# Where an odd tile's output projection transposes the next tile's inputs: behind two or behind three groups of products

## The chip, the cores and the metric

The kernel runs on one core of one Trainium2 chip. The time is that of one execution on the device, in microseconds (us), from several executions of which the median counts. The engines are named as in the profile: PE is TensorE (matrix products and transposes), ACT is ScalarE, DVE is VectorE, POOL is GpSimd, and SP is SyncE, which here only issues DMAs.

## The reference

The reference is one encoder layer over 2048 tokens of width 1024. Two kinds of attention give 512 columns each; these are normalised, joined and multiplied by one output matrix; the result is added to the residual stream; a router then picks two of 32 experts for each token, and their gated MLPs are added.

```python
mixed = concatenate([rmsnorm(out_a, g_out_a), rmsnorm(out_b, g_out_b)], axis=-1)
x = x + mixed @ w_out                                  # output projection, this change
h2 = rmsnorm(x, g_ffn_norm)
y = hierarchical_moe(h2, w_router_group, ..., w_gate, w_up, w_down)
x = x + y
return rmsnorm(x, g_final)
```

## The kernel before

The program is written out by hand: every engine executes its instructions in the order in which the code issues them, and an instruction whose input is not ready holds all that stands behind it on its engine. The change is in `phase5`, which does the output projection, the second norm and the routing, for 16 tiles of 128 tokens. Its loop body for tile n does pieces of several tiles:

- `proj(n)`: the products of tile n with the output matrix, two halves of 512 columns. Inputs and weights are split into a high and a low part, so each half takes three groups of eight products (high by high, high by low, low by high), six groups in all, numbered 1 to 6 here. `proj` is a generator; `ahead(pj, k)` issues the next k groups. The products are line L1425, with `mT_hi` or `mT_lo` as the input. The row of group 3 and of group 6 is thus one with `mT_lo`.
- `trans(n + 1)`: transposes the next tile's normalised inputs `ab` (PE, L1408, eight transposes, four to a PSUM tile), then takes each PSUM tile out in two steps: `mT_hi` on ACT (L1410) and `mT_lo` on DVE (L1411). `mT_hi` and `mT_lo` are needed by group 1 of the next tile.
- `trans2(n - 1)`: transposes the new residual stream of the tile before for the router (PE, L1477), taken out by ACT (L1483) and DVE (L1484) into `hT`.
- `resid`, `square`, `resid2`, `norm2`: residual addition (DVE, L1435), its squares (ACT, L1449), a Newton iteration for the inverse root (`nw`, first on DVE, then six small steps on POOL, L1295 and L1296), and the norm itself (DVE, L1466).
- `merge1` to `merge3`, `squares`, `rms`, `scale`: they make `ab` of later tiles. `rms` (a second Newton iteration, for two tiles, all on DVE, up to L1300) comes once in every even tile. `scale` (two ACT steps, L1353, one for each half of `ab`) writes `ab` of tile n + 2: in an even tile behind `rms`, near the end of the tile, in an odd tile right behind `trans2`. There is one `ab` buffer, so the next can be written only when the transposes have read the last.
- `logits` (even tiles, PE L1509 and L1511) and `route` (DVE steps, and POOL DMAs that write the routing table, L1616), dealt out a few steps at a time by `some(k)`. A table of four tiles starts in tiles 5, 9 and 13.

Both kinds of transposes take their PSUM tile from one pool `pt` (name `pT`) of two buffers, each holding four transposes:

```python
pt = cps.enter_context(tc.tile_pool(name="p5t", bufs=2, space=PSUM))
def ahead(it, k):
    for _ in range(k):
        next(it, None)
```

So the eight transposes of `trans` fill both buffers, and the eight of `trans2` behind them can start when DVE has finished the first `mT_lo`, and their second four when it has finished the second.

Of the kernel before, what the change touches and what calls it, by code (L numbers as in the profile page):

```python
# [36 lines left out]
class K:  # L37
# [1328 lines left out]
    def phase5(self):  # L1366
# [14 lines left out]
        with ExitStack() as ctx:  # L1381
# [15 lines left out]
            def load_x(c):  # L1397
                st[c]["x1"] = w2.tile([128, D], F32, name="x")
                nc.sync.dma_start(st[c]["x1"], x[c])

            def trans(c):
                d = st[c]
                ab = d.pop("ab")
                mT = d["mT"] = [wk.tile([128, 8, 128], F32R, name="mT_hi"), wk.tile([128, 8, 128], F32R, name="mT_lo")]
                for q in range(2):
                    ps = pt.tile([128, 4, 128], F32, name="pT")
                    for j in range(4):
                        nc.tensor.transpose(ps[:, j], ab[:, q, j], self.ident)  # L1408
                    sl = slice(4 * q, 4 * q + 4)
                    nc.scalar.activation(mT[0][:, sl], ps, AF.Copy)  # L1410
                    nc.vector.tensor_sub(mT[1][:, sl], ps, mT[0][:, sl])  # L1411

            def proj(c):

                d = st[c]
                mT = d.pop("mT")
                last = c == NT - 1
                t = [pm.tile([128, 2, 512], F32, name="pm") for _ in range(2 if last else 1)]
                d["ps"] = ps = [t[0][:, 0], t[1][:, 0]] if last else [t[0][:, 0], t[0][:, 1]]
                d["pt"] = t[0]  # L1420
                for half in range(2):
                    n = 0
                    for a, b in PASS:
                        for j in range(8):
                            nc.tensor.matmul(ps[half], mT[a][:, j], wo[b][j // 2][:, j % 2, 512 * half:512 * half + 512],  # L1425
                                             start=(n == 0), stop=(n == 23))
                            n += 1
                            if j == 7 or j == 3 and half and last:
                                yield

            def resid(c, half=None):
                d = st[c]
                x1 = d["x1"]
                if half is None:
                    nc.vector.tensor_add(x1, d["pt"].rearrange("p a b -> p (a b)"), x1)  # L1435
                else:
                    n = slice(512 * half, 512 * half + 512)
                    nc.vector.tensor_add(x1[:, n], d["ps"][half], x1[:, n])
                if half != 0:
                    nc.sync.dma_start(dr["x1"][128 * c:128 * c + 128], x1)  # L1440

            def square(c, half=None):
                d = st[c]
                if half is None:
                    d["h2"] = p.tile([128, 8, 128], F32, name="h2")
                if half != 1:
                    d["ssx"] = sm.tile([128, 2], F32, name="ssx")
                if half is None:
                    nc.scalar.activation(d["h2"].rearrange("p a b -> p (a b)"), d["x1"], AF.Square,  # L1449
                                         accum_out=d["ssx"][:, 0:1])  # L1450
                else:
                    nc.scalar.activation(d["ps"][half], d["x1"][:, 512 * half:512 * half + 512], AF.Square,
                                         accum_out=d["ssx"][:, half:half + 1])

            def resid2(c):
                d = st[c]
                ss = d.pop("ssx")
                if c == NT - 1:
                    nc.vector.tensor_add(ss[:, 0:1], ss[:, 0:1], ss[:, 1:2])
                d["rx"] = newton(ss[:, 0:1], 1.0 / D, sm, "nw2", last=c >= NT - 3)  # L1460
# [328 lines left out]
            def some(k):  # L1789

                nonlocal hold
                if hold:
                    hold -= 1
                    if hold:
                        return
                    if n == 14:
                        k = 100
                for _ in range(2 * k if 13 <= n < 15 else k):
                    if next(routes, None) == "pe":
                        hold = 4  # L1800
                        return

            def until(mark):
                nonlocal hold
                held, hold = hold, 0
                if held and mark == "pe":
                    return
                for m in routes:
                    if m is not None and m == mark:
                        break  # L1810
# [3 lines left out]
# [4 lines that stand above are left out]
            def finish_logits(n):  # L1818
                nonlocal routes
                for _ in lgs:  # L1820
                    pass
                g = {5: 0, 9: 1, 13: 2}.get(n)
                if g is not None:
                    until(None)
                    routes = chain(route(g), choose()) if g == 1 else route(g)
# [4 lines left out]
            def whole_w(e, m, t):  # L1830

                stages[e, 2 * m], stages[e, 2 * m + 1] = t[:, 0:1024], t[:, 1024:2048]
                gather(t, wsrc[m], self.idx2[:, e:e + 1])
# [38 lines left out]
            for n in range(NT - 1):  # L1872
                pj = proj(n)
                even = n % 2 == 0
                ahead(pj, 1)
                if n >= 1:
                    resid(n - 1)
                    square(n - 1)
                if not even and n >= 3:
                    finish_logits(n)  # L1880
                ahead(pj, 1)
                load_x(n)
                if even and n + 3 < NT:
                    load_ob(n + 3)
                if even and n + 2 < NT:
                    merge3(n + 2)
                    merge3(n + 3)
                some(4)
                trans(n + 1)
                if n >= 1:  # L1890
                    resid2(n - 1)
                some(4)
                if n == 12:
                    until(None)
                    whole_w(0, 0, self.slot(7, F32))
                    gu0 = [pA.tile([128, 4, 2, 256], F32R, name=f"a{i}") for i in range(4)]
                ahead(pj, 2)
                if n >= 1:
                    trans2(n - 1)
                if even and n + 2 < NT:  # L1900
                    squares(n + 2)
                    squares(n + 3)
                if n + 5 < NT:
                    load(n + 5)
                if not even and n + 2 < NT:
                    scale(n + 2)
                    if n + 3 < NT:
                        load_ob(n + 3)
                if n == 13:
                    half_split(0, 0, (gu0,), nc.vector)  # L1910
                if n == 14:
                    for i in (2, 3):
                        half_split(0, i, (gu0,), nc.vector)
                some(3)
                if n + 4 < NT:
                    merge1(n + 4)
                if n >= 1:
                    norm2(n - 1)
                some(2)
                if n + 4 < NT:  # L1920
                    merge2(n + 4)
                some(2)
                if even:
                    for _ in pj:
                        pass
                    if n >= 2:
                        lgs = logits(n - 1)
                        next(lgs)
                if even and n + 2 < NT:
                    rms(n + 2)  # L1930
                    scale(n + 2)
                if n == 13:
                    half_split(0, 1, (gu0,), nc.vector)
                if n == 13:
                    whole_w(0, 1, self.slot(7, F32))
                if n == 13:
                    for i in range(3):
                        half_w(1, i, self.stage())
                if n == 14:
                    until(None)  # L1940
                    first_rec()
                some(2)
                for _ in pj:
                    pass

            n = NT - 1
            pj = proj(n)
# [464 lines left out]
```

## Time and profile before

| what | value |
| --- | --- |
| time, median of 3 runs | 2306.95 us (2306.91 to 2308.32) |
| profiled execution, its own time | 2312.83 us |
| span of the profiled execution | 2310.6 us |
| PE busy, share of the span | 2060.5 us, 89% |
| DVE, ACT, POOL busy | 1666.5, 1439.9, 1092.7 us |
| the loop over tiles 0 to 15 | about 1500 to 1790 us of the span |

The span is counted from the first to the last instruction; the profiled execution's own time is 2.2 us longer, and it lies 5.9 us above the median of the runs without a profile. A change of the profiled execution is therefore carried over to the median as a difference. Rows of a timeline give the start, the duration, the engine, the line, the operation, output and inputs, the shape and a count where equal instructions are merged; in brackets stands how long the engine was idle before the row, and which instruction ended that. A PE row's duration reaches to the modelled end of its last product, which overlaps the start of the next row, so the time that a row takes is read from start to start.

### The profile page before, as it was taken

The page shows a single profiled execution, that of the slowest core. Times are in us where ns is not written, and L with a number is a line of the kernel's source. Part 1 is how long each engine was busy: PE and PEld are TensorE (multiplying, and loading weights), DVE is VectorE, ACT ScalarE, POOL GpSimd, SP SyncE. Part 2 cuts the span into 40 slices and gives each one's busy share as a digit, 9 for nine tenths or more (in the row PEclk, how much of TensorE's full clock was granted, in tenths as well). Part 3 has the DMA queues.
Part 4 walks back from the last instruction along what each step waited for, and adds up shares of the span by engine and source line. Part 5 has one row for each costly group of instructions (what it writes and reads, how often), then busy time and mean ns, then how long its engine had stood idle before and what let it go on. Part 6 is the DMA issues. An engine that isn't in the chain of part 4 may idle for free. (4 is left out here: it accounts for less than half of the span.)

```text
span 2310.6 us, 42905 instructions
## 1 busy us (share of the span) xinstructions
PE 2060.5 (89%) x16099; PEld 1458.3 (63%) x16099; DVE 1666.5 (72%) x3741; ACT 1439.9 (62%) x2125; POOL 1092.7 (47%) x1193
## 2 busy tenths in 40 slices
PE   5889989788889899999999999898888899999990
PEld 3458434577778466665655655577776588788870
DVE  7732221488887788888888899968787577777765
ACT  5532211499997588888888878744343366667653
POOL 1110000377763255555555556644654656667740
PEclk9989989999999899999999999899998999999995
DMA  4412344956735100000000221154444789999978
GB/s 153 131 54 68 123 151 122 224 139 153 163 100 154 37 20 22 6 22 21 7 22 9 55 93 24 34 165 143 150 147 147 219 298 293 291 308 319 311 211 308
DMA packets 196676, 312.81 MB, mean 135 GB/s; under 512 B 64185, under 2 KB 149090, under 8 KB 183460
## 3 DMA queue, kind: packets, MB, share of 16 engines
q1 hardware_dynamic: 166420, 174.43, 26.4%
q0 software_dynamic: 29760, 134.85, 18.2%
q8 instruction: 127, 2.08, 0.4%
q14 instruction: 81, 0.66, 0.1%
q10 hardware_dynamic: 288, 0.79, 0.1%
HBM read 235.66 MB, written 101.25 MB: 146 GB/s over the span
## 5 line engine op out<-in xcount | busy, mean ns | idle before, releaser
L961 POOL TENSOR_TENSOR lo<-p,hi 128x512 f16<-128x512 f32 x256 | 343.0, 1344 | 295.5 <-ACT p L955 233.7
L954 ACT ACTIVATE hi<-S,mla_scale 128x1024 f16<-128x1024 f32 x256 | 285.5, 1115 | 135.0 <-PE S L949 133.4
L923 DVE TENSOR_REDUCE part<-M 128x1 f32<-128x512 f32 x512 | 340.4, 680 | 13.1 <-PE M L921 11.7
L955 ACT ACTIVATE p<-S,mla_scale 128x1024 f32<-128x1024 f32 x256 | 285.2, 1114 | 0.0
L960 DVE TENSOR_TENSOR lo<-p,hi 128x512 f16<-128x512 f32 x256 | 228.9, 895 | 12.1 <-ACT p L955 10.3
L983 PE MATMUL O<-VB,lo 128*128 128x65 f16 x2048 | 198.9, 194 | 6.8 <-DVE lo L960 4.3
L978 PEld LDWEIGHTS <-hi 128*128 128x128 f16 x2048 | 184.9, 98 | 27.0 <-issue 21.5
L978 PE MATMUL O<-VB,hi 128*128 128x129 f16 (+1 forms) x2048 | 198.9, 215 | 0.0
L983 PEld LDWEIGHTS <-lo 128*128 128x128 f16 x2048 | 177.7, 99 | 17.4 <-DVE lo L960 5.9
L729 POOL TENSOR_TENSOR pp<-sb,st 128x256 f32<-128x256 f32 (+1 forms) x256 | 142.9, 581 | 45.1 <-DVE st L706 32.9
L2117 DVE TENSOR_TENSOR s<-raw,s 128x1024 fp32r<-128x1024 f32 x120 | 140.2, 1221 | 17.1 <-ACT s L2115 16.0
L1425 PE MATMUL pm<-s,mT_hi 128*128 128x512 f32 x512 | 137.3, 415 | 3.8 <-ACT mT_hi L1410 3.8
L2074 PE MATMUL pd<-s,hT 128*128 128x512 f32 x540 | 138.2, 404 | 1.7 <-ACT hT L2061 1.7
L614 POOL TENSOR_SCALAR t<-t,a_scale 128x512 f32<-128x512 f32 (+1 forms) x12 | 16.1, 1354 | 261.3 <-DMA t<-d_r 245.2
L2161 POOL DMA_INDIRECT d_x<-o,rec x47 | 88.1, 1874 | 106.7 <-ACT s L2115 33.7
L365 DVE SCALAR_TENSOR_TENSOR qk_sb<-pm,wscale,qk_sb 128x512 f16<-128x512 f32 x32 | 24.0, 750 | 149.3 <-ACT qk_sb L364 149.3
L746 PE MATMUL PT<-ident,pp 128*128 128x128 f32 (+1 forms) x640 | 104.5, 287 | 25.6 <-ACT pp L733 24.0
L2115 ACT ACTIVATE s<-raw 128x1024 fp32r<-128x1024 f32 x120 | 118.2, 1049 | 12.8 <-DMA raw<-in_w_up,eidx 6.8
L733 ACT ACTIVATE pp<-pp,a_scale 128x512 f32<-128x512 f32 (+1 forms) x160 | 114.0, 713 | 11.2 <-POOL pp L729 9.5
L2074 PEld LDWEIGHTS pd<-s,hT 128*128 128x128 f32 x540 | 101.2, 188 | 30.1 <-issue 4.3
L364 ACT ACTIVATE qk_sb<-pm,wscale 128x512 f16<-128x512 f32 x32 | 22.0, 688 | 153.4 <-DMA d_qk<-qk_sb 76.8
L1425 PEld LDWEIGHTS pm<-s,mT_hi 128*128 128x128 f32 x512 | 98.8, 198 | 26.1 <-ACT mT_hi L1410 4.1
(511 smaller groups left out, 5963.7 us busy)
## 6 DMA issues: line engine op xcount, KB each, us to landing
x<-in_x SPq DMA_DIRECT2D x32, 512.0 KB
na<-d_na SPq DMA_DIRECT2D x48, 264.0 KB
d_qk<-qk_sb SPq DMA_DIRECT2D x64, 128.0 KB
d_x<-x SPq DMA_DIRECT2D x16, 512.0 KB
d_h<-h SPq DMA_DIRECT2D x16, 512.0 KB
y<-d_x SPq DMA_DIRECT2D x16, 512.0 KB
out<-y SPq DMA_DIRECT2D x16, 512.0 KB
d_q<-qs SPq DMA_DIRECT2D x16, 384.0 KB
```

Of the source, the lines that this page charges most:

```text
L729: nc.gpsimd.tensor_sub(dst, src, res[:, s0 + i, 65:66, None, None].to_broadcast([128, 2, na, nx // 2]))
L923: nc.vector.tensor_reduce(part[m][:, qt, kc:kc + 1], ps, axis=AX.X, op=ALU.max)
L954: nc.scalar.activation(hi, ps, AF.Exp, scale=es)
L955: nc.scalar.activation(p32, ps, AF.Exp, scale=es)
L960: nc.vector.tensor_sub(lo[:, :, 0:LV], p32[:, :, 0:LV], hi[:, :, 0:LV])
L961: nc.gpsimd.tensor_sub(lo[:, :, LV:512], p32[:, :, LV:512], hi[:, :, LV:512])
L978: nc.tensor.matmul(o[:, c0:c0 + own], hi[:, j, q], V[:, 0:own], start=(kt == 0 and qt == 0), stop=False, skip_group_check=True)
L983: nc.tensor.matmul(o[:, c0:c0 + 65], lo[:, j, q], V[:, 0:65], start=False, stop=(kt == 15 and qt == 3), skip_group_check=True)
L1425: nc.tensor.matmul(ps[half], mT[a][:, j], wo[b][j // 2][:, j % 2, 512 * half:512 * half + 512], start=(n == 0), stop=(n == 23))
L2074: self.nc.tensor.matmul(ps[:, half], hT[a][:, j], w[b][:, j, 512 * half:512 * half + 512], start=(n == 0), stop=(n == len(k) - 1))
L2115: nc.scalar.activation(hi, src, AF.Copy)
L2117: eng.tensor_sub(lo, src, hi)
```

## The change

In odd tiles group 3 is issued ahead of `trans(n + 1)`, and only group 4 between `trans(n + 1)` and `trans2(n - 1)`. In even tiles nothing changes. The condition covers tiles 1, 3, 5, 7, 9, 11 and 13; tile 15 has its own code behind the loop.

```diff
                 some(4)
+                if not even:
+                    ahead(pj, 1)
                 trans(n + 1)
                 if n >= 1:
                     resid2(n - 1)
...
-                ahead(pj, 2)
+                ahead(pj, 2 if even else 1)
                 if n >= 1:
                     trans2(n - 1)
```

PE's rows of tile 1, as a piece of the difference; `pm` is the sum of the products, `ab` the input of tile 2, and the two first rows are the end of group 2.

```order
 L1425 MATMUL pm<-s_21031,mT_hi 128x512 x2
 L1425 MATMUL pm<-s_21101,mT_hi 128x512 x2
-L1408 MATMUL pT<-ident,ab 128x128 x8
 L1425 MATMUL pm<-s_20018,mT_lo 128x512 x2
 L1425 MATMUL pm<-s_20185,mT_lo 128x512 x2
 L1425 MATMUL pm<-s_20352,mT_lo 128x512 x2
 L1425 MATMUL pm<-s_20523,mT_lo 128x512 x2
+L1408 MATMUL pT<-ident,ab 128x128 x8
 L1425 MATMUL pm<-s_20018,mT_hi 128x512 x2
 L1425 MATMUL pm<-s_20185,mT_hi 128x512 x2
```

The eight transposes of `ab` have moved behind the eight products of group 3 (`mT_lo`); nothing else has moved.

PE's rows of tile 5 before, from the end of group 2 to the transposes of `trans2(4)` (`x`):

```order
L1425 MATMUL pm<-s_21101,mT_hi 128x512 x2
L1408 MATMUL pT<-ident,ab 128x128 x8
L1425 MATMUL pm<-s_20018,mT_lo 128x512 x2
L1425 MATMUL pm<-s_20185,mT_lo 128x512 x2
L1425 MATMUL pm<-s_20352,mT_lo 128x512 x2
L1425 MATMUL pm<-s_20523,mT_lo 128x512 x2
L1425 MATMUL pm<-s_20018,mT_hi 128x512 x2
L1425 MATMUL pm<-s_20185,mT_hi 128x512 x2
L1425 MATMUL pm<-s_20352,mT_hi 128x512 x2
L1425 MATMUL pm<-s_20523,mT_hi 128x512 x2
L1477 MATMUL pT<-ident,x 128x128 x8
```

The same stretch of the changed kernel:

```order
L1425 MATMUL pm<-s_21101,mT_hi 128x512 x2
L1425 MATMUL pm<-s_20018,mT_lo 128x512 x2
L1425 MATMUL pm<-s_20185,mT_lo 128x512 x2
L1425 MATMUL pm<-s_20352,mT_lo 128x512 x2
L1425 MATMUL pm<-s_20523,mT_lo 128x512 x2
L1408 MATMUL pT<-ident,ab 128x128 x8
L1425 MATMUL pm<-s_20018,mT_hi 128x512 x2
L1425 MATMUL pm<-s_20185,mT_hi 128x512 x2
L1425 MATMUL pm<-s_20352,mT_hi 128x512 x2
L1425 MATMUL pm<-s_20523,mT_hi 128x512 x2
L1477 MATMUL pT<-ident,x 128x128 x8
```

Between the two sets of transposes there are now eight products instead of sixteen. ACT, DVE, POOL and SP issue the same instructions in the same order as before; only buffer numbers and line numbers behind the edit differ.

## Rows read from the trace of the kernel before

**Rows 1.** Waits, tiles 0 to 15: us in total, times, longest.
```profile
PE pT L1408 <- ACT ab L1353: 14.6, 12, 5.3
```

**Rows 2.** Timeline of PE, tile 4, an even tile.
```profile
1568.03 1.03 PE L1408 MATMUL pT<-ident,ab 128*128 128x128 f32 x8
1568.82 2.13 PE L1425 MATMUL pm<-s,mT_lo 128*128 128x512 f32 x8
...
1572.65 1.03 PE L1477 MATMUL pT<-ident,x 128*128 128x128 f32 x8
```

**Rows 3.** Timeline of PE, tile 5, and in the last row tile 6.
```profile
1585.66 0.66 PE L1408 MATMUL pT<-ident,ab 128*128 128x128 f32 x4 [2.45 <-ACT ab L1353]
1586.62 0.66 PE L1408 MATMUL pT<-ident,ab 128*128 128x128 f32 x4 [0.30 <-ACT ab L1353]
1587.04 3.39 PE L1425 MATMUL pm<-s,mT_lo 128*128 128x512 f32 x8
...
1592.40 1.03 PE L1477 MATMUL pT<-ident,x 128*128 128x128 f32 x8
...
1608.99 1.97 PE L1477 MATMUL pT<-ident,x 128*128 128x128 f32 x8 [3.48 <-DVE mT_lo L1411]
```

**Rows 4.** Timeline of DVE, tile 5, and in the last row tile 6.
```profile
1588.13 1.29 DVE L1411 TENSOR_TENSOR mT_lo<-pT,mT_hi 128x512 fp32r<-128x512 f32 x2 [0.87 <-ACT mT_hi L1410]
...
1593.66 1.29 DVE L1484 TENSOR_TENSOR hT<-pT,hT 128x512 fp32r<-128x512 f32 x2 [2.80 <-ACT hT L1483]
...
1608.26 1.27 DVE L1411 TENSOR_TENSOR mT_lo<-pT,mT_hi 128x512 fp32r<-128x512 f32 x2
```

**Rows 5.** Timeline of PE, tile 3 and tile 9.
```profile
1553.40 2.07 PE L1408 MATMUL pT<-ident,ab 128*128 128x128 f32 x8 [2.38 <-ACT ab L1353]
...
1559.69 1.03 PE L1477 MATMUL pT<-ident,x 128*128 128x128 f32 x8
...
1657.07 2.07 PE L1408 MATMUL pT<-ident,ab 128*128 128x128 f32 x8 [5.29 <-ACT ab L1353]
...
1662.35 2.14 PE L1425 MATMUL pm<-s,mT_hi 128*128 128x512 f32 x8
1664.33 1.03 PE L1477 MATMUL pT<-ident,x 128*128 128x128 f32 x8
```

**Rows 6.** Stretches: length, busy time of PE, PEld, DVE, ACT, POOL, granted clock, DMA.
```profile
1518.00:1532.00 14.00, 13.39 (x66) 10.56 (x65) 8.75 (x25) 7.32 (x11) 3.59 (x8) 1.00 0.54 158
1553.40:1558.00 4.60, 4.59 (x17) 3.86 (x18) 2.42 (x10) 2.82 (x5) 0.34 (x1) 0.63 0.83 267
1618.50:1632.90 14.40, 13.59 (x69) 10.71 (x68) 11.19 (x44) 7.69 (x12) 6.58 (x11) 1.00 0.57 166
1627.30:1646.70 19.40, 19.40 (x101) 16.08 (x100) 13.02 (x24) 9.24 (x20) 16.76 (x23) 1.00 0.60 177
1657.00:1662.00 5.00, 4.93 (x16) 4.01 (x17) 3.80 (x19) 2.98 (x7) 0.47 (x2) 0.50 0.84 236
```

**Rows 7.** Timeline of DVE, `norm2` in tile 8 and in tile 12.
```profile
1646.72 2.35 DVE L1466 SCALAR_TENSOR_TENSOR h<-x,nw,gf 128x1024 f32<-128x1024 f32 x1 [2.25 <-POOL nw L1296]
...
1719.49 2.30 DVE L1466 SCALAR_TENSOR_TENSOR h<-x,nw,gf 128x1024 f32<-128x1024 f32 x1 [2.88 <-POOL nw L1296]
```

**Rows 8.** Timeline of PE, tile 13.
```profile
1726.70 2.11 PE L1425 MATMUL pm<-s,mT_lo 128*128 128x512 f32 x8
...
1730.52 1.04 PE L1477 MATMUL pT<-ident,x 128*128 128x128 f32 x8
```

**Rows 9.** Timeline of DVE, tile 13.
```profile
1727.95 1.28 DVE L1411 TENSOR_TENSOR mT_lo<-pT,mT_hi 128x512 fp32r<-128x512 f32 x2
...
1735.22 1.23 DVE L1851 TENSOR_TENSOR a<-s,a 128x1024 fp32r<-128x1024 f32 x1 [1.80 <-ACT a L1849]
```

**Rows 10.** Groups of instructions, tiles 0 to 15: busy, mean ns, idle before.
```profile
L1616 POOL DMA_INDIRECT d_tab<-rec,ix x30 | 40.2, 1340 | 29.5 <-DVE ix L1613 22.5 <-issue 5.8 <-DVE nw L1288 0.3
```

**Rows 11.** Timeline of POOL, tile 8.
```profile
1646.83 3.71 POOL L1616 DMA_INDIRECT d_tab<-rec,ix  x1
```

## Prediction

> **What bounds the kernel now.** I read the waits of the 290 us in which the sixteen tiles of the output projection run, then PE's timeline there, then DVE, ACT and POOL around each of PE's gaps. PE is the engine with the most work, so a gap of PE there costs time unless something else holds the next step anyway. The largest wait of PE is the one that the change touches: the transposes of the next tile's inputs wait 14.6 us in 12 pieces for ACT's `ab` [rows 1]. In the timeline all of them lie in odd tiles. Even tiles have none: tile 4 goes from group 2 straight into the transposes, which take 0.79 us from start to start, and the two groups behind them 3.83 us, so 1.92 us a group [rows 2].
>
> Tile 5 shows the pattern. PE sits idle for 2.45 us, transposes the first half, waits 0.30 us for the second half of `ab`, and starts group 3 at 1587.04 [rows 3]. Group 3 itself needs nothing of this; it only stands behind. The gap also costs clock: behind 2.38 us of idle time in tile 3 the granted clock averages 0.63 over the next 4.6 us, behind 5.29 us in tile 9 it is 0.50, and in tiles 1 and 7, where PE idles 0.61 and 0.81 us in all, it stays at 1.00 [rows 5, 6]. 1.00 is 2.4 GHz and 0.50 is 1.2 GHz.
>
> **What the change does.** It issues no instruction more or less. Eight products with their weight loads move ahead of eight transposes, in seven tiles. No DMA moves, and SP's and POOL's queues keep their order; ACT and DVE keep theirs too. So there are two effects: 1.92 us of work lies in the gap, and one group less lies between `trans` and `trans2`, which makes `trans2` come sooner after the transposes but also gives ACT and DVE only one group's time to empty the two PSUM buffers.
>
> I follow each odd tile to the start of `trans2`, since what DVE and ACT do behind it starts from there.
>
> *Tile 5.* `ab` does not come sooner, since its makers stand before the edit, so the transposes still start at 1585.66 and 1586.62; the gap before them shrinks from 2.45 to about 0.5 us. Group 4 can start 0.42 us behind the second four, at 1587.04, at full clock since the long gap is gone, and ends 1.92 us later: `trans2` at 1588.96 instead of 1592.40, 3.4 us sooner [rows 3]. Are the buffers empty? The two `mT_lo` start at 1588.13 and take 1.29 us together, so the first buffer is free at about 1588.8 and the second at 1589.4 [rows 4]; the second four transposes are due at about 1589.4. This costs 0.1 us at most. But DVE was idle for only 2.80 us before it took `hT` [rows 4], so DVE's work moves up by 2.8 us, not 3.4. It then runs without a gap to `mT_lo` of tile 6 at 1608.26, for which PE waits 3.48 us [rows 3, 4]. DVE decides there: tile 5 gives 2.8 us.
>
> *Tile 3.* The same spacing (0.96 between the halves, 0.42, 1.92) puts `trans2` 3.3 us behind the transposes instead of 6.29 us (1553.40 to 1559.69) [rows 3, 5]: 3.0 us.
>
> *Tile 1.* PE idles 0.61 us in the whole tile [rows 6], all of it less than a group: 0.6 us.
>
> *Tile 7.* Its gap is 0.81 us [rows 6] and goes too, but the next odd tile does not feel it. `norm2` in tile 8 waits 2.25 us for the Newton steps on POOL [rows 7], and POOL is busy for 16.76 of the 19.40 us before that [rows 6], back to the Newton steps of tile 7, which start from that tile's `mT_lo`. That `mT_lo` does not come sooner, rather 0.2 us later, as the transposes now stand behind group 3. So `ab` of tile 10, behind that `norm2` on DVE, comes when it came. Tile 7 gives nothing that lasts.
>
> *Tile 9.* The transposes start at 1657.07 as before. PE has been idle 3 us or more even with group 3 done, so I let them and group 4 run at the low clock, as the transposes and group 3 did: `trans2` starts at 1662.35 instead of 1664.33 [rows 5]. 2.0 us.
>
> *Tiles 11 and 13.* Again `norm2` of tile 12 waits for POOL, 2.88 us [rows 7], so tile 11, whose gap is like tile 7's, gives nothing that lasts. In tile 13 group 4 starts at 1726.70, where group 3 did, and `trans2` could start at 1728.6; but DVE, busy with routing steps, ends the second `mT_lo` at 1729.2 [rows 8, 9], so the second four transposes start at about 1729.3 instead of 0.4 us behind 1730.52: 1.6 us. DVE's next large step, L1851, waits 1.80 us for ACT [rows 9], and ACT's copy stands behind the evictions of `trans2`, so most of it passes: 1.5 us.
>
> **The sum**: 0.6 + 3.0 + 2.8 + 0 + 2.0 + 0 + 1.5 = 9.9 us. What follows, the expert phase and the final norm, is started by instructions behind these, so I count the shift one to one. The profiled execution would take 2312.83 - 9.9 = 2302.9 us; the median lies 5.9 us below the profiled time, so the forecast is 2306.95 - 9.9 = **2297.0 us**.
>
> The upper bound of the gain: if POOL does not hold tiles 9 and 13, the gaps of tiles 7 and 11 count as well (0.8 each) and tile 13 gets the whole group of 1.9; with the 0.6 us that DVE takes back in tile 5 this is 9.9 + 1.6 + 0.4 + 0.6 = 12.5, and with a warm start in tile 9 (group 4 in 1.92 instead of twice that) some 14 us. The lower bound is the first rival.
>
> **The rivals.**
>
> *POOL is held longer.* With `trans2` sooner, DVE's `norm2` and merges of tiles 7 and 11 move against POOL's table DMAs, which stay. Such a DMA takes 1.34 us on the mean, but 3.71 us where `norm2` started 0.1 us ahead of it [rows 7, 10, 11]. If one more is held so in each of the pairs 7 to 9 and 11 to 13, `ab` comes 2.4 us later there: 9.9 - 4.8 = 5.1 us gained, 2301.8 us. For it: POOL's chain has no slack in these two stretches. Against it: DVE only moves up by about 1 us, and a DMA that is held early may escape being held later. The Trainium skill, page "SBUF — State Buffer", section "Who interferes with whom", says why such a thing can be: VectorE and GpSimd share one pair of ports, whichever starts first has it for its whole instruction, and the other is blocked entirely. By that rule it would be a matter of who comes first, so the sign is open. The one long DMA here agrees with it; no row shows which port was held.
>
> *It changes nothing.* If POOL and DVE set the pace in every pair of tiles as they do from 7 on, only a gap here and there counts: 0 to 4 us, 2303 to 2307 us. Against it: from tile 1 to tile 5 the waits of DVE are for ACT's `hT`, so for PE (2.80 us in tile 5) [rows 4].
>
> *`trans2` waits for the buffers.* This ends slower. One group gives ACT and DVE 0.79 + 1.92 = 2.7 us from the first transpose until `trans2` wants the first buffer. If `mT_lo` comes as late as in tile 6, where PE waits 3.48 us with two groups in between [rows 3], the wait comes in odd tiles too, and groups 5 and 6 and all behind are held. It decides from 9.9 / 7 = 1.4 us more wait in each odd tile on; with 2.1 us more the kernel is 4.8 us slower, 2311.8 us. Against it: in tile 5 `mT_lo` ends 2.8 us behind the second four transposes [rows 3, 4], in tile 13, where DVE is behind, I find 0.6 us.
>
> *POOL does not hold at all*: the upper bound, 2293 to 2294.5 us.
>
> **How the numbers follow.** The main case, 2294.5 to 2299.5 us, gets 58 in 100; POOL held longer, 2299.5 to 2302.5 us, 20; the upper bound 9; no change 9; slower 4. A change under 0.2% (4.6 us) counts as none, which is about what a measurement here can tell. Faster by more than that are the first three, 0.87; within it 0.09; slower 0.04. The range 2293.5 to 2302.0 us holds the main case, nearly all of the first rival and a part of the upper bound, some 8 in 10.
>
> **What the changed profile would show.** PE's wait at L1408 for `ab` falls from 14.6 us to about 5, most of it in tile 9. The clock behind tiles 3 and 5 stays at 1.00. In tiles 3 and 5 `trans2` starts 3.3 us behind the first transposes, and its own wait for `mT_lo` in odd tiles is under 1 us in all. Tile 6 and tile 10 keep a wait for `mT_lo` of 3.5 us or more. The stretches between `trans` of tiles 7 and 9, and of 11 and 13, keep their length. The prediction fails if POOL's chain moves by more than 2 us in either direction, if `trans2` in odd tiles waits over 1 us each, or if the expert phase gives the shift back.

## The result and the profile after

The changed kernel takes 2293.88 us in the median of six runs (2292.35 to 2297.93), the kernel before 2306.81 us in six (2300.94 to 2308.32). The ratio is 0.9949, with a 95% interval of 0.9935 to 0.9963, which is 8.5 to 15.0 us less; the medians differ by 12.9 us, and 9.9 us were forecast. The profiled span is 2291.1 us against 2310.6, so 19.5 us less, but half of this lies ahead of the change: the first transposes of `ab` in tile 0 start at 1489.6 us instead of 1499.5, and nothing ahead of them was edited. In the eleven profiles of this study that start lies between 1489.5 and 1499.5 us. I therefore measure the change on a **stage** of the trace, from the start of these first transposes to the start of the first transposes of `xa` behind tile 15: 270.1 us before and 261.4 us after. Behind the stage 541.0 us follow before and 540.1 us after: the expert phase gives nothing back.

The waits of the changed kernel between 1500 and 1790 us, in us in total, times and longest, answer to [rows 1]:

```profile
DVE nm L1327 <- POOL na L1322: 13.1, 4, 5.8
...
PE pT L1477 <- DVE mT_lo L1411: 11.9, 5, 3.9
...
PE pT L1408 <- ACT ab L1353: 7.0, 7, 4.7
```

PE's wait for `ab` is halved, from 14.6 to 7.0 us, and 4.7 us of what is left is tile 9. The wait of `trans2` for `mT_lo` grew from 8.7 to 11.9 us. DVE's wait for POOL's merge is 13.1 us; it was 2.8 us before, and 5.6 us in the second profile of the kernel before (c0_before below).

PE's timeline in tile 5, and in the last row tile 6, answers to [rows 3]:

```profile
1571.85 0.66 PE L1408 MATMUL pT<-ident,ab 128*128 128x128 f32 x4 [0.62 <-ACT ab L1353]
1572.81 0.66 PE L1408 MATMUL pT<-ident,ab 128*128 128x128 f32 x4 [0.30 <-ACT ab L1353]
1573.22 2.11 PE L1425 MATMUL pm<-s,mT_hi 128*128 128x512 f32 x8
1575.17 1.14 PE L1477 MATMUL pT<-ident,x 128*128 128x128 f32 x8
...
1592.27 1.97 PE L1477 MATMUL pT<-ident,x 128*128 128x128 f32 x8 [3.88 <-DVE mT_lo L1411]
```

The gap fell from 2.45 to 0.62 us, and `trans2` starts 3.32 us behind the first transposes instead of 6.74. Its duration of 1.14 instead of 1.03 us is all that the two PSUM buffers cost here. In tile 6 the wait for DVE rose from 3.48 to 3.88 us, since PE gained more than DVE.

The stretches behind the transposes of tiles 3, 5 and 9 (columns as in [rows 6]):

```profile
1542.50:1547.10 4.60, 4.28 (x26) 3.56 (x27) 2.44 (x10) 3.46 (x7) 0.33 (x1) 1.00 0.81 263
1571.80:1576.20 4.40, 4.05 (x25) 3.26 (x26) 3.23 (x15) 3.36 (x7) 0.00 (x0) 1.00 0.81 244
1641.30:1646.30 5.00, 4.95 (x16) 4.09 (x17) 3.79 (x19) 2.96 (x6) 0.50 (x2) 0.52 0.84 252
```

In tiles 3 and 5 the granted clock is 1.00, the higher of the two levels, where the kernel before had 0.63 in tile 3. In tile 9, where 4.67 us of idle time are left, it is still low, 0.52.

### The profile page after: what moved, and what is told of

Its sections match the earlier page's. It is cut to its first block, busy times and chain, and to the rows that moved or that the text cites. A ratio compares the mean times of both kernels' runs of the same rounds, so it can differ in the third digit from the quotient of the medians.

```text
span 2291.1 us, 42906 instructions
## 1 busy us (share of the span) xinstructions
PE 2049.4 (89%) x16099; PEld 1448.3 (63%) x16099; DVE 1657.7 (72%) x3741; ACT 1438.2 (63%) x2125; POOL 1096.3 (48%) x1193
## 5 line engine op out<-in xcount | busy, mean ns | idle before, releaser
L2163 POOL DMA_INDIRECT d_x<-o,rec x47 | 83.1, 1768 | 109.3 <-ACT s L2117 32.6
L2076 PEld LDWEIGHTS pd<-s,hT 128*128 128x128 f32 x540 | 101.1, 188 | 30.4 <-issue 4.3
```

What stands on the lines that cost most here:

```text
L2076: self.nc.tensor.matmul(ps[:, half], hT[a][:, j], w[b][:, j, 512 * half:512 * half + 512], start=(n == 0), stop=(n == len(k) - 1))
```

## The experiments

All of them are read in one table: the stage cut at the starts of `trans2` of tiles 1, 3, 6, 10 and 14, as they stand in PE's timelines. For instance 46.4 for tiles 4 to 6 of the changed kernel is 1592.27 - 1545.84. A segment holds the odd tiles named in it and ends where the next chain starts.

| kernel | tiles 0, 1 | 2, 3 | 4 to 6 | 7 to 10 | 11 to 14 | to `xa` | stage |
| --- | --- | --- | --- | --- | --- | --- | --- |
| before | 28.0 | 32.2 | 49.3 | 71.9 | 64.7 | 24.0 | 270.1 |
| c0_before, the same again | 28.8 | 32.1 | 49.4 | 71.9 | 66.5 | 24.2 | 272.8 |
| changed | 27.0 | 29.3 | 46.4 | 70.7 | 64.4 | 23.6 | 261.4 |
| c1_after, the same again | 27.8 | 29.3 | 46.3 | 70.6 | 64.9 | 24.0 | 262.8 |
| e1_t35 | 28.8 | 29.3 | 46.5 | 71.7 | 66.4 | 24.0 | 266.7 |
| e2_t711 | 28.7 | 32.1 | 49.2 | 72.3 | 67.3 | 24.2 | 273.9 |
| e6_t913 | 28.0 | 32.3 | 49.4 | 70.7 | 63.5 | 24.2 | 268.1 |
| e3_two | 28.1 | 29.3 | 46.8 | 71.9 | 66.9 | 23.7 | 266.8 |
| e4_all | 28.8 | 29.3 | 46.4 | 72.0 | 64.3 | 24.0 | 264.9 |
| e7_nwonly | 28.0 | 32.3 | 49.3 | 69.2 | 62.1 | 24.0 | 264.9 |
| e5_nwdve | 27.0 | 29.3 | 46.4 | 66.8 | 60.7 | 24.0 | 254.1 |

The segments of tiles 2 to 10 repeat within 0.2 us between two profiles of one kernel. Those of tiles 0, 1 and of tiles 11 to 14 do not. Runs e1, e2, e4 and e6 have one execution each, so they are read by these segments and not by their times.

**The kernel before once more (c0_before).**

> A control: the kernel before, unchanged. The stage is measured in the trace, from the first of PE's transposes of ab (tile 0) to the first transposes of xa behind tile 15: 270.1 us in the profile of before (1499.5 to 1769.6), 261.4 us in that of the changed kernel. Theory: the stage repeats within 1 us, and what lies ahead of it, which the edit does not touch and which was 9.8 us shorter in the changed kernel's profile, moves by several us from execution to execution. Rival: the edit shortens the part ahead too; then this run's stage starts at 1499 again.

Measured: ratio 0.9999 (0.9985 to 1.0014), stage 272.8 us, started at 1498.0. Whether an edit behind the part ahead of the stage can shorten that part stays open: the nine edited copies start their stages at 1489.5 to 1496.5, and both profiles of the kernel before come later, at 1498.0 and 1499.5. Against it speaks that the edited copies differ by 7 us among themselves, and that the kernel before alone takes 2300.3 to 2315.7 us in its runs. The stage starts behind this part, so its length does not hang on the answer. That the stage repeats within 1 us was wrong: it is 2.7 us longer. Most of this is one gap. PE's timeline of this run in tile 13, against [rows 8]:

```profile
1724.42 0.66 PE L1408 MATMUL pT<-ident,ab 128*128 128x128 f32 x4 [1.53 <-ACT ab L1353]
1725.78 3.26 PE L1425 MATMUL pm<-s,mT_lo 128*128 128x512 f32 x8
1728.84 2.46 PE L1425 MATMUL pm<-s,mT_hi 128*128 128x512 f32 x8
1731.14 1.03 PE L1477 MATMUL pT<-ident,x 128*128 128x128 f32 x8
```

Behind a gap of 1.53 us group 3 takes 3.26 us here; in the first profile of the same kernel it takes 2.11 us in the same place.

**The changed kernel once more (c1_after).**

> A control: the changed kernel, unchanged. Theory: the stage repeats within 2 us of 261.4, its differences lying in tile 0 and in tiles 12 to 14, where the clock behind a short gap differs between executions; time 8 to 12 us below before. Rival (the stage of the first profile was a lucky one): 265 us or more.

Measured: ratio 0.9957 (0.9943 to 0.9971), stage 262.8 us. The mean of two stages of each kernel is 271.4 before and 262.1 after, so the change gives 9.4 us. The differences lie where the theory put them, in tiles 0 and 1 and in tiles 11 to 14.

**Tiles 3 and 5 alone (e1_t35).**

```diff
+                if n in (3, 5):
+                    ahead(pj, 1)
                 trans(n + 1)
...
-                ahead(pj, 2)
+                ahead(pj, 1 if n in (3, 5) else 2)
```

> The change in tiles 3 and 5 alone. Theory: each gives the group that fits in its gap and the clock that the gap cost; trans2 3.3 us behind the first transposes in both, 3.0 and 2.8 us gained, the stage 264.3 us. Rival (POOL or DVE sets the pace in tiles 7 to 13 whatever happens before): the stage 268 us or more.

Measured: one run of 2299.97 us, stage 266.7 us, 6.1 us under c0_before and 3.4 us under the first profile of before, so the whole stage does not decide. The segments do: tiles 2, 3 and 4 to 6 are as short as in the changed kernel (29.3 and 46.5 us), all others are those of c0_before within 0.2 us. The 2.8 and 2.9 us of tiles 3 and 5 stay until the end, and tile 9 then waits 6.3 us for `ab` but takes its usual time. The rival falls: POOL and DVE carry what came sooner on unchanged.

**Tiles 7 and 11 alone (e2_t711).** The edit is that of e1_t35 with `(7, 11)`.

> The change in tiles 7 and 11 alone. Theory: POOL's chain from the Newton steps of tile 7 to norm2 of tile 8 decides when tile 9 can transpose, so trans2 of tiles 7 and 11 comes 1.2 us sooner and PE's wait for ab in tiles 9 and 13 grows by as much; the stage 270 us, no gain. Rival (POOL holds nothing): 1.2 us lasting from each, the stage 267.7 us.

Measured: one run of 2306.35 us, stage 273.9 us, 1.1 us above c0_before. `trans2` of tile 7 does come 1.3 us sooner after that of tile 6 (17.9 against 19.2 us), but the whole segment up to tile 10 is 0.5 us longer. PE's timeline in tile 9:

```profile
1649.23 2.07 PE L1408 MATMUL pT<-ident,ab 128*128 128x128 f32 x8 [6.66 <-ACT ab L1353]
```

The wait in tile 9 is 6.66 us, against 5.6 us in c0_before. The rival is out: nothing lasts, as the theory has it. The edit even costs something: 0.5 us in tiles 7 to 10, and 0.9 us in tiles 11 to 14 against e1_t35 and c0_before, in which the clock fell in tile 13 as it does here. The longer wait in tile 9 alone does not show POOL's chain at work: in e1_t35 it is 6.3 us with tile 7 as before.

**Tiles 9 and 13 alone (e6_t913).** The edit is that of e1_t35 with `(9, 13)`.

> The change in tiles 9 and 13 alone. Theory: tile 9 gives 2.0 us (a group in its long gap, group 4 at the low clock) and tile 13 1.0 to 1.5 us (a group in its gap, less what mT_lo on DVE is late); the stage 266.6 to 267.1 us, trans2 of tile 9 5.3 us behind its transposes. Rival (tiles 9 and 13 gain only because tiles 3 and 5 come sooner): the stage 269 us or more.

Measured: one run of 2298.79 us, stage 268.1 us. Tiles 7 to 10 take 1.3 us less than before, not 2.0: `trans2` stands 4.9 us behind the transposes of tile 9, but these start 49.2 us behind `trans2` of tile 6 instead of 48.1, though tiles 7 and 8 are not edited here. Tiles 11 to 14 take 1.2 us less than in the first profile of before and 2.9 us less than in c0_before, where the clock fell in tile 13. So these tiles gain by themselves, as the theory has it; for tile 13 the size is open by as much as the clock varies.

**Two groups in the gap (e3_two).**

```diff
+                if not even:
+                    ahead(pj, 2)
                 trans(n + 1)
...
-                ahead(pj, 2)
+                ahead(pj, 2 if even else 0)
```

> In odd tiles groups 3 and 4 both ahead of the transposes of the next tile, so that trans2 stands right behind them. Theory (the two PSUM buffers are next): in tiles 1, 7 and 11, which have hardly a gap, trans2 waits about 1.3 us for mT_lo, and the later mT_lo puts off POOL's chain and with it ab of tiles 9 and 13 by up to 1.9 us; tile 9 gains 2 us of group 4 in its gap; tiles 3 and 5 as in the changed kernel. The stage 263 to 266 us, 2 to 4 us above the changed kernel. Rival (the buffers cost nothing): tile 9's gap takes the second group and the stage falls to 259.5 us.

Measured: ratio 0.9985 (0.9971 to 0.9999), stage 266.8 us, 4.0 to 5.4 us above the changed kernel. The theory was right in direction, and the loss is larger than the 2 to 4 us that it gave: `trans2` waits about 1 us for `mT_lo` in all seven odd tiles, not in three. As it said, POOL's chain is put off: `norm2` of tile 8 starts 40.5 us behind `trans2` of tile 6, against 38.7 in the changed kernel. PE's waits for `ab` nearly vanish (1.9 us), and its wait for `mT_lo` becomes 19.2 us in 12 pieces. PE's timeline in tiles 7 and 8:

```profile
1610.63 1.03 PE L1408 MATMUL pT<-ident,ab 128*128 128x128 f32 x8
1612.64 1.25 PE L1477 MATMUL pT<-ident,x 128*128 128x128 f32 x8 [0.98 <-DVE mT_lo L1411]
...
1628.10 1.25 PE L1477 MATMUL pT<-ident,x 128*128 128x128 f32 x8 [2.13 <-DVE mT_lo L1411]
```

With nothing between the two sets of transposes, the second waits 0.98 us for the first PSUM buffer in tile 7. In odd tiles one group between them is enough, and it is what the change leaves.

**Even tiles too (e4_all).**

```diff
                 some(4)
-                if not even:
-                    ahead(pj, 1)
+                ahead(pj, 1)
                 trans(n + 1)
...
-                ahead(pj, 2 if even else 1)
+                ahead(pj, 1)
```

> Group 3 ahead of the transposes of the next tile in even tiles too. Theory: even tiles have no gap before these transposes; PE reaches trans2 at the same time as before, and DVE, which takes mT_lo late there anyway, ends it before trans2 wants the buffer in tiles 2, 4, 8 and 12, so the stage stays within 1 us of the changed kernel's 261.4. Rival (one group is too short for the evictions wherever DVE is busy): 0.7 us or more lost in each of six even tiles, the stage 265 us or more.

Measured: one run of 2298.89 us, stage 264.9 us, 2.1 to 3.5 us above the changed kernel's two. Neither forecast holds as a whole. In tiles 2 to 6 and 11 to 14 the segments are those of the changed kernel, as the theory said; tiles 0 and 1 take 1.0 to 1.8 us more, and tiles 7 to 10 1.4 to 1.5 us more. PE's timeline in tile 8 shows the second:

```profile
1628.44 1.03 PE L1408 MATMUL pT<-ident,ab 128*128 128x128 f32 x8
1629.23 2.12 PE L1425 MATMUL pm<-s,mT_hi 128*128 128x512 f32 x8
1633.50 1.25 PE L1477 MATMUL pT<-ident,x 128*128 128x128 f32 x8 [2.15 <-DVE mT_lo L1411]
```

DVE is late there because POOL is: behind `norm2` of tile 7 a table DMA starts 0.11 us after it and takes 4.29 us, where in the changed kernel it starts 0.07 us ahead of it and takes 1.03 us, and DVE then waits 5.79 us for POOL's merge. So there is nothing to win in even tiles, and where DVE is late there is something to lose.

**The Newton steps of four tiles on DVE, without the change (e7_nwonly).** The edit is in `resid2`:

```diff
-                d["rx"] = newton(ss[:, 0:1], 1.0 / D, sm, "nw2", last=c >= NT - 3)
+                d["rx"] = newton(ss[:, 0:1], 1.0 / D, sm, "nw2", last=c >= NT - 3 or c in (6, 7, 10, 11))
```

> The kernel before, with only the Newton steps of four tiles on DVE instead of POOL (tiles 7, 8, 11 and 12), no group moved. Theory: POOL's chain is what makes ab late in tiles 9 and 13, so PE's longest wait for ab falls from 5.3 to 5.6 us to about 3 us, tile 9 (trans2 of tile 8 to trans2 of tile 9) from 23.1 to about 20 us; tiles 3 and 5 keep their waits of 2.4 us; the stage 3 to 5 us below before, 267 us. Rival (the Newton steps help only where the group has moved): within 1 us of before, 270 to 272.8 us.

Measured: ratio 0.9960 (0.9944 to 0.9975), stage 264.9 us, 5.2 and 7.9 us below the two profiles of before and so more than the theory gave. Tiles 7 to 10 take 2.7 us less and tiles 11 to 14 2.6 to 4.4 us less; all other segments are those of before. PE's timeline in tile 9:

```profile
1647.19 0.65 PE L1408 MATMUL pT<-ident,ab 128*128 128x128 f32 x4 [3.05 <-ACT ab L1353]
```

The wait is 3.05 us instead of 5.29 [rows 5]. POOL's chain is what makes `ab` late in tiles 9 and 13.

**The change and the Newton steps together (e5_nwdve).** Both edits.

> The change, and besides the six Newton steps of norm2 for the tiles whose norm2 comes in tiles 7, 8, 11 and 12 on DVE instead of POOL. Theory (POOL holds tiles 9 and 13): norm2 of tile 8 no longer waits 2 to 4 us for POOL, PE's wait for ab in tile 9 falls from 4.7 to about 2.5 us and the one in tile 13 is gone, the stage 257.5 to 259.5 us. Rival (DVE holds them): 1.5 us more work on DVE in each of four tiles, the stage 261 to 265 us.

Measured: 2289.25 us in the median of four runs, ratio to before 0.9905 (0.9875 to 0.9934), stage 254.1 us, better than the theory by 3.4 us: 7.3 us under the first profile of the changed kernel, all of it in tiles 7 to 14. By ratio and by stage this version beats both kernels. PE's wait in tile 9 falls to 1.84 us, but the clock still falls behind it:

```profile
1642.17 0.65 PE L1408 MATMUL pT<-ident,ab 128*128 128x128 f32 x4 [1.84 <-ACT ab L1353]
...
1643.53 3.47 PE L1425 MATMUL pm<-s,mT_hi 128*128 128x512 f32 x8
1646.80 1.28 PE L1477 MATMUL pT<-ident,x 128*128 128x128 f32 x8
```

## Why the prediction was right

**The bound and the mechanism.** The gaps of PE in odd tiles cost time, a group put into them is worth its time and what the gap cost in clock, and DVE or POOL takes back a part. e1, e2 and e6 show this by pairs of tiles. The sum was 9.9 us; the two stages of each kernel give 9.4 us, and the two ratios hold 9.9 in their intervals. That the sum is so close is partly luck: two terms were about 1.2 us too large together, the others about 0.8 us too small.

**Term by term** (mean of two profiles of each kernel):

| term | forecast | measured |
| --- | --- | --- |
| tile 1 | 0.6 | 1.0 |
| tile 3 | 3.0 | 2.9 |
| tile 5, less what DVE takes back | 2.8 | 3.0 |
| tiles 7 and 9 | 0 + 2.0 | 1.3 |
| tiles 11 and 13 | 0 + 1.5 | 1.0 (0.4 and 1.6) |
| rest | 0 | 0.3 |

*Tiles 3 and 5* came out by their own steps: 3.3 us from the first transposes to `trans2`, the clock at its higher level, a trace of a wait at the buffers, and DVE as the limit of tile 6.

*Tile 1* was under-sized. I took PE's idle time in the tile, 0.61 us, but a PE row's modelled end overlaps the next row's start, so the idle time in the stretch is less than the start was late: the first transposes came 0.5 us behind the end of group 2 as read from start to start, and took 1.36 instead of 0.79 us because of the wait for the second half.

*Tiles 7 and 9* were over-sized by 0.7 us. `trans2` of tile 9 starts 5.0 and 4.9 us behind the first transposes instead of 7.3 and 7.0, so this step gives the 2.0 us that I priced. The step that did not hold is that `ab` of tile 10 comes when it came: the transposes of tile 9 start 49.1 us behind `trans2` of tile 6, and 48.1 and 48.3 before. POOL's chain is longer by 0.7 us: from the first Newton step of tile 7 to `norm2` of tile 8 it takes 19.4 us before (1627.31 to 1646.72) and 20.2 us after (1610.78 to 1630.93). But it is not shown that the change makes it longer. In e1 and e6, where tiles 7 and 8 are those of before, the chain takes 20.3 us too, and the transposes of tile 9 start at 48.9 and 49.2. The difference there is one table DMA of POOL, which starts 1.1 us into `norm2` of tile 7 in all four; it takes 2.02 and 2.04 us in the two profiles of before, 3.29 in e1 and 3.27 in e6. Before, and in e6:

```profile
1632.36 2.02 POOL L1616 DMA_INDIRECT d_tab<-rec,ix  x1 [0.30 <-issue]
```

```profile
1622.73 3.27 POOL L1616 DMA_INDIRECT d_tab<-rec,ix  x1 [0.30 <-issue]
```

Nor is it shown that the late `ab` costs the 0.7 us: in e1 it is late as well, `trans2` then stands only 6.2 us behind the transposes, and tiles 7 to 10 take no longer than before. So where the 0.7 us went stays open. The 0 for tile 7 held: tiles 7 to 10 take 70.7 us in e6, without the edit in tile 7, and 70.7 and 70.6 us in the changed kernel, with it; in e2 it costs 0.5 us. POOL's timeline in tiles 7 and 8 of the changed kernel:

```profile
1613.27 1.03 POOL L1616 DMA_INDIRECT d_tab<-rec,ix  x1 [0.15 <-issue]
1614.61 3.14 POOL L1616 DMA_INDIRECT d_tab<-rec,ix  x1 [0.30 <-DMA ob<-d_ob]
```

and DVE's:

```profile
1613.34 2.35 DVE L1466 SCALAR_TENSOR_TENSOR h<-x,nw,gf 128x1024 f32<-128x1024 f32 x1
1615.56 1.35 DVE L1319 TENSOR_TENSOR na<-na,nm 128x520 f32<-128x520 f32 x2
1616.78 1.26 DVE L1435 TENSOR_TENSOR x<-pm,x 128x1024 f32<-128x1024 f32 x1
...
1622.92 0.21 DVE L1327 RECIPROCAL nm<-na 128x8 f32<-128x8 f32 x1 [4.50 <-POOL na L1322]
```

The first table DMA starts 0.07 us ahead of `norm2` and takes 1.03 us. The second starts while DVE runs `norm2`, and ends 0.84 us behind the end of DVE's merges (L1319), at 1616.91. A second path that I had not named leads on from there: DVE waits 4.50 us for POOL's merge before it can take `mT_lo` of tile 8, and `trans2` of tile 8 then waits 0.58 us. That wait of `trans2` is not there in e1 and e6, and it is in c1_after (0.56 us). In tile 12 the same wait is 2.02 us in both profiles of the changed kernel.

*Tiles 11 and 13.* Here the change does make POOL's chain longer: from tile 11's first Newton step to `norm2` of tile 12 it takes 21.2 us in both profiles of the changed kernel and in e2, and 20.2 to 20.3 us in before, c0_before, e1 and e6. `norm2` of tile 11 starts 20.7 us behind `trans2` of tile 10 instead of 22.3, now 0.11 us ahead of the first of three table DMAs, where before only the third one started behind it:

```profile
1683.79 4.30 POOL L1616 DMA_INDIRECT d_tab<-rec,ix  x1
```

The longest one there took 3.23 us before; in c1_after it takes 4.29 and in e2 4.31 us. So the first rival, that POOL is held longer, came true in one of its two pairs of tiles, with 1.0 us instead of the 2.4 us that I priced. Its cost shows against e6, which leaves tile 11 as it was: tiles 11 to 14 take 63.5 us there, and 64.4 and 64.9 in the changed kernel. The 0 for tile 11 was therefore too good by about 1 us; what tile 13 gives by itself varies with the clock behind its gap.

**The other rivals.** That nothing changes is out by the ratio, and by e1. That `trans2` waits for the buffers is out for the change: its five waits for `mT_lo` (11.9 us) all lie in even tiles. e3 shows that it is real one group further. That POOL does not hold is out by e7, in which `ab` of tiles 9 and 13 comes sooner with no group moved and only the Newton steps of four tiles taken off POOL, and by e2.

**What the changed profile was to show.** `ab` wait about 5 us: 7.0, most of it in tile 9. Clock 1.00 behind tiles 3 and 5: yes. Waits in tiles 6 and 10 of 3.5 us or more: 3.88 and 3.44. The stretch between the transposes of tiles 7 and 9 unchanged: 34.0 us before, 33.7 after, because both ends come about 1 us later; of tiles 11 and 13: 30.4 and 31.3, in c1_after 32.6, so this one did not keep its length.

## What to carry to other kernels

A gap of an in-order engine can be filled by moving independent work ahead of the instruction that waits, but what it gains must be followed to the next thing that decides: here it was worth its full size in tiles 3 and 5, two thirds of it in tile 9, and nothing or less where another engine's chain set the next wait. Count what the move takes away behind the waiting instruction too: in odd tiles one group between two uses of a pair of PSUM buffers was enough, none was not. And when a gap remains with the filler in place, look at the chain that ends it: moving 24 tiny steps from POOL to DVE gave two thirds of what the change gave (stage 6.6 against 9.4 us). And before a difference of 1 us is put down to an edit, look whether the same stretch shows it in copies that the edit does not touch.

## What the runs showed of the hardware

The clock behind a gap of the same length is not the same in each execution: behind 1.54 us the granted clock was 1.00 over the next 4.6 us in the first profile of before, and behind 1.53 us 0.72 in the second (c0_before):

```profile
1725.30:1729.90 4.60, 4.27 (x22) 3.44 (x23) 4.22 (x20) 2.95 (x6) 0.07 (x1) 1.00 0.88 359
```

```profile
1724.40:1729.00 4.60, 4.28 (x17) 3.38 (x18) 4.22 (x20) 2.94 (x6) 0.08 (x1) 0.72 0.90 342
```

That is 1.5 us in one tile. In e1_t35 it was 0.63 behind 1.51 us in tile 13, in e6_t913 1.00 behind 1.66 us in tile 11. So a gap of this length cost clock in some executions and not in others, while the longer ones (2.4 us and more, in tiles 3, 5 and 9 of before) cost it in both profiles, with 0.50 to 0.70.

A table DMA on POOL, 0.96 us alone, takes 2.0 to 4.4 us when it starts while DVE runs `norm2`. Where the hold ends is not the same in each execution. Where merges follow, it mostly ends 0.8 to 1.0 us behind their end, as in the rows above; in tile 7 of both profiles of before it ended 0.8 us behind the end of `norm2`, with the merges still to come; and in tile 8 the same program, the changed kernel, shows 3.02 us in one profile and 4.35 in the other, the DMA starting 0.1 us behind `norm2` in both. What decides this the runs do not show. When the DMA starts first it is not held: at 1613.27, 0.07 us ahead of `norm2`, it took 1.03 us. The Trainium skill, page "SBUF — State Buffer", section "Who interferes with whom", says that VectorE and GpSimd share a pair of ports, that whichever starts first keeps it for its instruction, and that a VectorE instruction with two inputs in SBUF contends with a GpSimd instruction that reads SBUF. The trace agrees with the order of starts deciding: 1.03 us when the DMA came 0.07 us ahead in tile 7, 4.30 us when it came 0.11 us behind in tile 11. Which port it is no run here shows.

The part ahead of the stage, the same instructions in all eleven profiles, varies by 10 us, and the part behind it by 6 us (535.4 to 541.4). This is as large as the change; without a stage that is measured in the trace, single profiles would have told nothing.
